# A SiLU-multiply kernel on one core: the body as one critical section with hand-written semaphores

## The chip, the cores and the metric

The kernel runs on one core of one Trainium2 chip. The metric is the device time in microseconds (us) of one execution. Before the change three executions took 471.06, 471.17 and 470.71 us; the median is 471.06.

The names of the engines in the profile: ACT is ScalarE, DVE is VectorE, POOL is GpSimd, SP is SyncE, and a q behind a name (SPq, ACTq) means the engine's sequencer, which issues DMAs and handles semaphores. This kernel does not use TensorE.

## The reference

The input has 32 x 512 rows of 2048 float32 numbers. Each row is split in two halves of 1024; the first goes through SiLU and is multiplied by the second. The output has the same rows with 1024 numbers each.

```python
x1, x2 = x[..., :half_dim], x[..., half_dim:]
silu_x1 = x1 * (1 / (1 + np.exp(-x1)))
return (silu_x1 * x2).astype(np.float32)
```

So 134.22 MB are read, 67.11 MB written, and each output element costs one activation and one multiply.

## The kernel before

The 16,384 rows are cut into 16 tiles of 1,024 rows. A tile holds K = 8 rows on each of the 128 partitions; two tiles (RUN = 2) share a group of rows, in which each partition owns 16 consecutive rows (`view`, line 42). There are two input buffers `xt` (64 KB for each partition) and two output buffers `ot` (32 KB for each partition); tile i uses buffer i % 2 of both.

For each tile:

- **load** (line 81): one DMA of 8 MB, issued by SP into `xt`, through the move helper, so that its line in the profile is L77.
- **compute** (line 91): ACT applies SiLU in place to the first half of each row in `xt` (L96); DVE multiplies it with the second half into `ot` (L102). A tile is one activation and one multiply of 128 x 8192 elements. Tile 0 is computed in four chunks of 2 rows (FIRST), the last tile in chunks of 2, 3 and 3 rows (LAST).
- **store** (line 109): one DMA of 4 MB, issued by ACT from `ot`, again L77. Tile 0 is stored by three DMAs over interleaved partitions (OPENING: every fourth from 0, every fourth from 2, every second from 1); the last tile by one DMA for each chunk.

Loads of tiles 0 and 1 come first. After that the load of tile i + 2 waits for tile i's multiply, which frees its input buffer, and the multiply of tile i waits for the store of tile i - 2, which frees its output buffer. Loads pass only through SP's DMA queue (q1 in the profile) and stores only through ACT's (q10).

The order of the work comes from three things. Within `manual_schedule` (line 45) ACT and DVE issue their instructions in the order in which the program writes them. All semaphores are set by the framework from the data that instructions share; it has one semaphore for each engine and a ring of eight for the DMAs, which the transfers take in turn. The kernel shapes these waits: `implied` (line 50) declares dependences that other waits already cover, so that no wait is made for them; `after` (line 58) fixes the order in which transfers take their semaphores (that order depends on `load_first`, line 125, which is true for tiles 4 to 7 and 12 to 15); and `settle_all_but` (line 66) gives SP an instruction that does nothing but wait for each earlier transfer and the last tile's multiplies ahead of the last transfer (its waits are on L67). At the end the framework waits on SP for what is still open and has all engines meet in a barrier, clear the semaphores and meet once more (these instructions are on L160, where its context closes). At the start all engines meet in a barrier as well (L149).

Of the kernel before, what the change touches and what calls it, by code (L numbers as in the profile page):

```python
# [1 line left out]

# [4 lines left out]


@with_exitstack
def kernel(  # L10
    ctx: ExitStack,
    tc: tile.TileContext,
    x: bass.AP,
    out: bass.AP,
):


    nc = tc.nc
    P = nc.NUM_PARTITIONS

    x_flat = x.flatten_outer_dims()
    out_flat = out.flatten_outer_dims()
    num_rows, in_cols = x_flat.shape
    half = in_cols // 2
    dt = x_flat.dtype

    K = 8
    FIRST = [2] * (K // 2)
    LAST = [2, 3, 3]
    OPENING = [  # L30
        (slice(0, None, 4), slice(None)),
        (slice(2, None, 4), slice(None)),
        (slice(1, None, 2), slice(None)),
    ]
    RUN = 2
    n_tiles = num_rows // (P * K)

    pool = ctx.enter_context(tc.tile_pool(name="pool", bufs=1))
    xts = [pool.tile([P, K, in_cols], dt, name=f"xt{b}") for b in range(2)]
    ots = [pool.tile([P, K, half], dt, name=f"ot{b}") for b in range(2)]  # L40

    def view(flat, i):
        return flat.rearrange("(g p t k) d -> g t p k d", p=P, t=RUN, k=K)[i // RUN, i % RUN]

    ctx.enter_context(tc.manual_schedule(engines={mybir.EngineType.Activation, mybir.EngineType.DVE}))

    sent = []
    loads, stores, silus, muls = {}, {}, {}, {}

    def implied(later, earlier, reason):  # L50
        for x in later:
            for y in earlier:
                tc.declare_no_dep(x, y, reason=reason)

    def earlier(done, i):
        return [ins for j in range(i % 2, i, 2) for ins in done[j]]

    def after(later, first):
        tc.add_manual_dep(
            later,  # L60
            first.name,
            mybir.DependencyInfo(mybir.DependencyClass.NoSync, mybir.DependencyReason.DATA),
            reason="order in which the transfers take their semaphores",
        )

    def settle_all_but(n, others):
        rest = nc.sync.nop(nofuse=True)  # L67
        for ins in sent[:-n] + others:
            tc.add_manual_dep(
                rest.ins,  # L70
                ins.name,
                mybir.DependencyInfo(mybir.DependencyClass.Sync, mybir.DependencyReason.DATA),
                reason="sync sees each earlier transfer land before the last ones",
            )

    def move(queue, out, in_):
        ins = queue.dma_start(out=out, in_=in_).ins  # L77
        sent.append(ins)
        return ins

    def load(i):
        loads[i] = [move(nc.sync, xts[i % 2][:], view(x_flat, i))]
        if i >= 2:
            implied(loads[i], earlier(loads, i), "the multiplies that this load awaits came after those loads")
            implied(loads[i], earlier(silus, i), "the multiplies that this load awaits came after those activations")

    def parts(sizes):
        assert sum(sizes) == K
        return [slice(sum(sizes[:n]), sum(sizes[:n + 1])) for n in range(len(sizes))]

    def compute(i, ot, chunks):
        xt = xts[i % 2]
        silus[i], muls[i] = [], []
        for ks in chunks:
            silus[i].append(
                nc.scalar.activation(  # L96
                    out=xt[:, ks, :half],
                    in_=xt[:, ks, :half],
                    func=mybir.ActivationFunctionType.Silu,
                ).ins  # L100
            )
            muls[i].append(nc.vector.tensor_mul(out=ot[:, ks], in0=xt[:, ks, :half], in1=xt[:, ks, half:]).ins)  # L102
        implied(muls[i], loads[i], "each multiply awaits an activation that came after the load")
        if i >= 2:
            implied(silus[i], earlier(silus, i), "the load that this activation awaits came after those activations")
            implied(silus[i], earlier(muls, i), "the load that this activation awaits came after those multiplies")
            implied(muls[i], earlier(muls, i), "the store that this multiply awaits came after those multiplies")

    def store(i, ot, pieces):
        ov = view(out_flat, i)  # L110
        stores[i] = [move(nc.scalar, ov[ps, ks], ot[ps, ks]) for ps, ks in pieces]

    ALL = slice(None)
    load(0)
    load(1)
    for i in range(n_tiles):
        ot = ots[i % 2]
        last = i == n_tiles - 1
        compute(i, ot, parts(FIRST if i == 0 else LAST if last else [K]))
        pieces = [(ALL, ALL)]  # L120
        if i == 0:
            pieces = OPENING
        elif last:
            pieces = [(ALL, ks) for ks in parts(LAST)]
        load_first = i // 4 % 2
        if load_first and i + 2 < n_tiles:
            load(i + 2)
        store(i, ot, pieces)
        if load_first and i + 2 < n_tiles:
            after(stores[i][0], loads[i + 2][0])  # L130
        if not load_first and i + 2 < n_tiles:
            load(i + 2)
            after(loads[i + 2][0], stores[i][-1])
    settle_all_but(1, muls[n_tiles - 1])


# [1 line left out]
_INS = ['x']  # L138
_OUTS = [((32, 512, 1024), 'float32')]


# [23 lines left out]
```

## Time and profile before

| what | us |
|---|---|
| median of the three times | 471.06 (470.71 to 471.17) |
| span of the profiled execution, first to last instruction | 469.19 |
| between the two: time around the span | 1.87 |
| ACT busy | 114.2 (24%) |
| DVE busy | 139.5 (30%) |
| share of the 16 DMA engines: loads, stores | 66.4%, 33.2% |
| activation of 128 x 8192 (L96), mean of 14 | 7.03 |
| multiply of 128 x 8192 (L102), mean of 14 | 8.69 |
| load of 8 MB, issue to landing, median | 42.2 |
| store of 4 MB, issue to landing, median | 42.0 |
| time of two tiles in the middle (one load issue to the next of the same buffer) | 58.0 |

The span runs from the program's first instruction to its last. The profiled execution is listed by its span alone; its own time lies above the span by about as much as the timed runs do, 1.87 us by their median. All times within the profile are counted from the start of the span.

How to read it: the page begins with the busy time of each engine, then gives the span in 40 equal slices with a digit for the busy share of each in tenths, and the DMA engines in the same way. A table of stretches gives the same for windows that one chooses. The chain of waits follows the work that ended last back to its start. The DMA issues list how long a transfer took from its issue until its semaphore said that it had landed. A DMA's time to landing includes the time that it stood in its queue behind others.

### The profile page before, as it was taken

What the parts mean: (1) busy time and instruction counts of PE and PEld (TensorE: products, weight loads), DVE (VectorE), ACT (ScalarE), POOL (GpSimd) and SP (SyncE); (2) the same over time, 40 slices, a digit from 0 to 9 for tenths busy, and PEclk for the clock granted to TensorE, in tenths of its full rate; (3) what the DMA queues carried; (4) which work ended last, traced back from release to release, by engine and by line L of the source; (5) the groups of instructions that cost most, each with busy time, mean ns of one, the idle gap of its engine ahead of it and who ended that gap; (6) DMA issues with size and microseconds to landing.
All of it is one profiled execution on the core that took longest, in us unless ns stands there. A gap on an engine that the chain in (4) does not pass through costs nothing.

```text
span 469.2 us, 156 instructions
## 1 busy us (share of the span) xinstructions
DVE 139.5 (30%) x21; ACT 114.2 (24%) x22; POOL 0.2 (0%) x4
## 2 busy tenths in 40 slices
DVE  0070522407034070330704307042070520605152
ACT  1051405032050410504105050050501405014060
POOL 0000000000000000000000000000000000000000
DMA  8999999999999999999999999999999999999998
GB/s 358 447 447 374 475 402 433 416 492 402 411 439 486 408 402 447 475 419 402 444 439 458 402 436 413 492 402 416 433 486 408 402 447 475 419 402 444 450 402 358
DMA packets 4928, 201.33 MB, mean 429 GB/s; under 512 B 576, under 2 KB 576, under 8 KB 576
## 3 DMA queue, kind: packets, MB, share of 16 engines
q1 hardware_dynamic: 2304, 134.22, 66.4%
q10 hardware_dynamic: 2624, 67.11, 33.2%
HBM read 134.22 MB, written 67.11 MB: 429 GB/s over the span
## 4 chain that ended last, share of the span: by engine, by line
DMA 72%; DVE 14%; ACT 11%; DVEq 1%; issue 0%; SPq 0%
DMA xt<-in_x_dram 72%; DVE ot L102 14%; ACT xt L96 11%; DVEq L160 1%; SPq L77 0%
## 5 line engine op out<-in xcount | busy, mean ns | idle before, releaser
L102 DVE TENSOR_TENSOR ot<-xt 128x8192 f32<-128x8192 f32 (+2 forms) x21 | 139.5, 6659 | 320.8 <-ACT xt L96 320.8
L96 ACT ACTIVATE xt<-xt 128x8192 f32<-128x8192 f32 (+2 forms) x21 | 112.9, 5400 | 341.4 <-DMA xt<-in_x_dram 341.4
L96 ACT ACT_TABLE_LOAD x1 | 1.3, 1283 | 0.7 <-PEq L149 0.7
L149 POOL MEMSET const-bfloat16-1.0<- 128x1 bf16 x1 | 0.1, 102 | 0.0
L149 POOL MEMSET const-uint8-127<- 128x1 uint8 x1 | 0.1, 102 | 0.0
L149 POOL MEMSET const-float32-0.0<- 128x1 f32 x1 | 0.1, 99 | 0.2 <-issue 0.2
L149 POOL MEMSET const-float32-1.0<- 128x1 f32 x1 | 0.1, 99 | 0.0
## 6 DMA issues: line engine op xcount, KB each, us to landing
out_dram<-ot ACTq DMA_DIRECT2D x14, 4096.0 KB, 42.0
out_dram<-ot ACTq DMA_DIRECT2D x3, 1024.0 KB, 12.0
out_dram<-ot ACTq DMA_DIRECT2D x2, 1536.0 KB, 7.9
out_dram<-ot ACTq DMA_DIRECT2D x1, 2048.0 KB, 37.2
xt<-in_x_dram SPq DMA_DIRECT2D x16, 42.2
```

The lines of the kernel that those rows point to most:

```text
L96: nc.scalar.activation(out=xt[:, ks, :half], in_=xt[:, ks, :half], func=mybir.ActivationFunctionType.Silu,).ins
L102: muls[i].append(nc.vector.tensor_mul(out=ot[:, ks], in0=xt[:, ks, :half], in1=xt[:, ks, half:]).ins)
L149: nc = _bacc.Bacc("TRN2", target_bir_lowering=False, num_devices=1)
L160: with _tile.TileContext(nc) as tc:
```

## The change

The framework's scheduling of the body is replaced by one critical section. The body is written once, in order, and every wait is written by hand. There are six semaphores: `acted` counts activations and `multiplied` multiplies; `loaded` and `stored` exist once for each buffer, and each transfer adds 16. What each engine waits for:

- ACT waits for a tile's load before its first activation, and for the multiplies before a store.
- DVE waits for the earlier stores from the same output buffer before a tile's first multiply, and for the activation before each multiply.
- SP waits for all multiplies of tile i before it issues the load of tile i + 2.
- GpSimd waits at the end until both `stored` counts are complete; it is the engine on which the section ends (`sync_engine`), and its own drain at that end is left out (`no_gpsimd_drain`).

The sizes of the tiles, the chunks, the pieces of the opening and last stores and the queues of the DMAs are the same. `manual_schedule`, the declared dependences, the order of semaphore slots with `load_first`, and `settle_all_but` go. In every tile the load is now written after the store.

```diff
-    ctx.enter_context(tc.manual_schedule(engines={mybir.EngineType.Activation, mybir.EngineType.DVE}))
...
-    settle_all_but(1, muls[n_tiles - 1])
+    with tc.tile_critical(sync_engine=mybir.EngineType.Pool, no_gpsimd_drain=True):
+        acted = ctx.enter_context(nc.semaphore("acted"))
+        multiplied = ctx.enter_context(nc.semaphore("multiplied"))
+        loaded = [ctx.enter_context(nc.semaphore(f"loaded{b}")) for b in range(2)]
+        stored = [ctx.enter_context(nc.semaphore(f"stored{b}")) for b in range(2)]
+        sent = [0, 0]
+        n_silu = n_mul = 0
+        def load(i):
+            nc.sync.dma_start(out=xts[i % 2][:], in_=view(x_flat, i)).then_inc(loaded[i % 2], 16)
+        load(0)
+        load(1)
+        for i in range(n_tiles):
...
+            nc.scalar.wait_ge(loaded[i % 2], 16 * (i // 2 + 1))
+            for ks in chunks:
                 nc.scalar.activation(
...
+                ).then_inc(acted, 1)
+            if i >= 2:
+                nc.vector.wait_ge(stored[i % 2], sent[i % 2])
+            done = []
+            for ks in chunks:
+                n_silu += 1
+                nc.vector.wait_ge(acted, n_silu)
+                nc.vector.tensor_mul(out=ot[:, ks], in0=xt[:, ks, :half], in1=xt[:, ks, half:]).then_inc(multiplied, 1)
+                n_mul += 1
+                done.append(n_mul)
+            pieces = [(ps, ks, n_mul) for ps, ks in OPENING] if i == 0 else [(ALL, ALL, n_mul)]
+            if last:
+                pieces = [(ALL, ks, n) for ks, n in zip(chunks, done)]
...
+            for ps, ks, n in pieces:
+                if n != awaited:
+                    nc.scalar.wait_ge(multiplied, n)
+                    awaited = n
+                nc.scalar.dma_start(out=ov[ps, ks], in_=ot[ps, ks]).then_inc(stored[i % 2], 16)
+                sent[i % 2] += 16
+            if i + 2 < n_tiles:
+                nc.sync.wait_ge(multiplied, n_mul)
+                load(i + 2)
+        for b in range(2):
+            nc.gpsimd.wait_ge(stored[b], sent[b])
```

More of the change, by code (lines that the diff above doesn't have):

```diff
@@ L43, in view @@
         return flat.rearrange("(g p t k) d -> g t p k d", p=P, t=RUN, k=K)[i // RUN, i % RUN]
-    ctx.enter_context(tc.manual_schedule(engines={mybir.EngineType.Activation, mybir.EngineType.DVE}))
[L47 to L85, printed above, removed]
     def parts(sizes):
@@ L89, in parts @@
         return [slice(sum(sizes[:n]), sum(sizes[:n + 1])) for n in range(len(sizes))]
[L91 to L95, printed above, removed]
+    ALL = slice(None)
+    with tc.tile_critical(sync_engine=mybir.EngineType.Pool, no_gpsimd_drain=True):
[5 more added lines that the diff above has]
+        n_silu = n_mul = 0
+        after_mul = []
+        def load(i):
[3 more added lines that the diff above has]
+        for i in range(n_tiles):
+            xt, ot = xts[i % 2], ots[i % 2]
+            last = i == n_tiles - 1
+            chunks = parts(FIRST if i == 0 else LAST if last else [K])
+            nc.scalar.wait_ge(loaded[i % 2], 16 * (i // 2 + 1))
+            for ks in chunks:
                 nc.scalar.activation(
@@ L99, in compute @@
                     func=mybir.ActivationFunctionType.Silu,
[L100 to L133, printed above, removed]
@@ new lines @@
+            if last:
+                pieces = [(ALL, ks, n) for ks, n in zip(chunks, done)]
+            ov = view(out_flat, i)
+            awaited = 0
+            for ps, ks, n in pieces:
[7 more added lines that the diff above has]
+                load(i + 2)
```

## The prediction

> **What bounds the kernel now.** I read the page first, then the table of stretches, the DMA issues, the chain of waits and at last the records at both ends. From the page, the busy rows and the chain:
>
> ```profile
> span 469.2 us, 156 instructions
> DVE 139.5 (30%) x21; ACT 114.2 (24%) x22; POOL 0.2 (0%) x4
> DMA  8999999999999999999999999999999999999998
> q1 hardware_dynamic: 2304, 134.22, 66.4%
> q10 hardware_dynamic: 2624, 67.11, 33.2%
> DMA 72%; DVE 14%; ACT 11%; DVEq 1%; issue 0%; SPq 0%
> ```
>
> The engines work 30% and 24% of the span; the 16 DMA engines work all of it: loads (q1) 66.4% and stores (q10) 33.2% make 99.6%. The chain gives DVE 14% and ACT 11%, but that is one buffer's chain: while tile 14 is multiplied, the other buffer's load keeps the DMA engines busy. The table of stretches (last two columns: DMA share, GB/s) shows it:
>
> ```profile
> 61.00:119.00 58.00, 17.52 (x3) 14.06 (x2) 0.00 (x0) 1.00 1.00 434
> 119.00:400.00 281.00, 80.08 (x10) 70.29 (x10) 0.00 (x0) 1.00 1.00 435
> 448.00:460.00 12.00, 8.62 (x3) 7.22 (x3) 0.00 (x0) 1.00 1.00 431
> ```
>
> The DMA share is 1.00 at 434 to 435 GB/s even from 448 to 460, where the last tile is computed. So the time is three pieces: until the first packet, 201.33 MB of packets, and what follows the last landing. The packet records put the first packet at 1.73 us and the end of the last at 468.04, 466.3 us of the span's 469.19. At 434 GB/s throughout, the bytes would take 463.9; the other 2.4 lie at the start (slices of 325 and 379 GB/s from 2 to 6 us), at the opening stores (346 and 335 GB/s from 36 to 40) and in the uneven finish after 466.
>
> How much cover there is, from the timeline and the chain's end:
>
> ```profile
> 406.86 0.33 SPq L77 DMA_DIRECT2D xt<-in_x_dram  x1
> 453.35 0.34 ACTq L77 DMA_DIRECT2D out_dram<-ot  x1
> 457.07 3.60 ACTq L77 DMA_DIRECT2D out_dram<-ot  x2
> 406.86 42.19 DMA xt<-in_x_dram
> 457.04 3.27 DVEq L160
> ```
>
> The load of tile 15 is issued at 406.86; by the semaphore records the load ahead of it lands at 419.94. It could be issued 13.1 us later before the load queue ran out. At the end tile 14's store lands at 458.63 and tile 15's three pieces at 461.08, 464.74 and 468.38, each right behind the one before. The first packet follows an issue by 1.0 us (issue 0.73, packet 1.73), so the pieces, issued at 453.35, 457.07 and 460.33, could each come about 4.3, 3.0 and 3.4 us later without a gap.
>
> **What the change removes.** The waits of the sync queue, in us:
>
> ```profile
> SPq L77 <- DVE ot L102: 400.0, 14, 31.9
> SPq L67 <- DMA out_dram<-ot: 44.5, 1, 44.5
> SPq L67 <- DMA xt<-in_x_dram: 12.9, 1, 12.9
> SPq L160 <- DMA out_dram<-ot: 3.5, 1, 3.5
> ```
>
> SP's nop with its waits (L67) is done at 464.86, 3.5 us before the last landing, so its removal saves nothing; what is late next is the last landing, as now. SP's 12 and ACT's 3 separate semaphore instructions on L77 take 17 ns each, with 10 us and more to spare: nothing. The declared dependences and the order of semaphore slots are no instructions. In tiles 4 to 7 and 12 to 15 the load was written ahead of the store and now stands behind it, but loads go through SP's queue and stores through ACT's, both wait for the same multiply (406.86 and 406.87 above), and no transfer passes another in its queue.
>
> **What it adds inside.** Per tile a wait on ACT for the load and one for the multiply, on DVE one for the stores two tiles back and one for the activation, on SP one for the multiply; five more of the kind stand at the chunks of tiles 0 and 15. Today most of these conditions ride on the instruction itself, so each is either folded in again (nothing) or a separate instruction. The nearest rows are steps between neighbouring sequencer instructions at L160: SP 0.055 to 0.062 us, GpSimd 0.078, ACT 0.092, DVE 0.110. From landing to next load issue three of them follow one another: at most 0.055 + 0.092 + 0.110 = 0.26 us a tile, against 13.1 us of cover. Behind ACT's wait for the multiply are the store and the next activation, as now; behind DVE's wait for stores the multiply, and the stores have landed by then (the ones that tile 2 needs at 71.94, its activation starts at 72.15). So I count 0; if the cover were gone it would be 16 x 0.26 = 4.1 us. At the end two such steps a piece (0.2 us) stand against 3.0 us. The table load of ACT (1.28 us, now at 0.72) may come to stand behind the first wait for data. Then tile 0 ends 1.3 us later, and load 2 is issued at 34.8 instead of 33.5, while load 1 lands at 45.36: 10.5 us of cover are left, again 0.
>
> **What it adds at the start.** Nothing is outstanding when the section is entered, so each engine enters by itself. Between the opening barrier and load 0 I count one more SP step, 0.06 us. Bounds: nothing, and a whole barrier round, which in the rows of the end takes 0.46 us (GpSimd's release at 468.62 to its next at 469.08). I take the step, since nothing earlier is there to wait for.
>
> **What it adds at the end.** Now, from the instruction records: the last landing releases SP at 468.40, its two drains follow at 468.46 and 468.51, GpSimd sees them at 468.55, and two barrier rounds end at 469.19. The rows of that line:
>
> ```profile
> L160 POOLq EVENT_SEMAPHORE  x4: 17/17/17, 468.5 to 469.1; - x4
> L160 SPq EVENT_SEMAPHORE  x3: 17/17/17, 468.4 to 469.1; - x3
> L160 SPq DRAIN  x3: 7/7/7, 468.5 to 468.8; - x3
> L160 POOLq EVENT_SEMAPHORE_RANGE_CLEAR  x1: 93/93/93, 468.8 to 468.8; - x1
> ```
>
> In the changed kernel GpSimd is released instead. After its wait I count a branch out, a placeholder in its drain's stead and the section's end: 3 x 0.078 = 0.23 us. The other engines' drains at the section's end wait for compute that ended by 460.3, so they cost nothing. Then SP has to learn of it (GpSimd's release at 468.62 reached SP's wait at 468.665, 0.04) and goes on as today: +0.27, say 0.28. Bounds: if GpSimd joins the barrier straight from its wait, SP's three steps fall away, -0.15; if the end also needs a barrier round of its own, 0.28 + 0.46 = +0.74. I take 0.28, whose rows are those of this very place.
>
> [...]
>
> **Sum.** 469.19 + 0.06 + 0.28 = 469.53 of span. The median of the timed runs is 471.06, 1.87 above the span (the single times, 470.71 to 471.17, 1.5 to 2.0); I leave these 1.87 as they are: 469.53 + 1.87 = **471.4 us**.
>
> **The rivals.**
> 1. *The new steps take the place of the old* (folded waits, GpSimd straight into the barrier, or an edit that leaves the order of events as it is): +0 - 0.15, 470.9 to 471.1. For it: the same engine leads the barrier. Against it: a section's end is work that has to sit somewhere.
> 2. *Barrier rounds at entry and exit*: 0.46 + 0.74 = +1.2, 472.3. Against it: nothing is outstanding at the entry, and the exit is told to skip GpSimd's drain.
> 3. *Slower, by code that has to be fetched.* If the section's code is not on the engine when SP enters it or GpSimd leaves it, the fetch stands fully on the path: load 0 isn't out yet, and the last landing is past. Nearest rows: all 13 packets of the instruction queue lie before the span, those of 8 KB take 0.32 to 0.53 us, and a transfer's first packet came 1.0 us after its issue; one fetch is 1.4 us, an estimate from these. One gives 471.4 + 1.4 = 472.8, both 474.2. It decides from a single miss on, since 1.4 is over the 0.94 us that are 0.2%. For it: GpSimd would leave the section after hundreds of us of waiting. Against it: every stream is short (156 records for all engines), and no instruction packet falls inside the span of before.
> 4. *Faster*: the opening stores meet the loads otherwise and the dip at 36 to 40 us (0.86 us) goes, perhaps with the start's 0.75. 469.8 to 470.5. Against it: same three pieces, same queues, same trigger.
>
> [...]
>
> **How the numbers follow.** Forecast 0.72, rival 1 0.12, rival 2 0.06, rival 3 0.06, rival 4 0.04. A measurement of this kernel can tell about 0.2%, 0.94 us, from no change: 470.12 to 472.00. Forecast and rival 1 lie inside, and rival 4 with its first dip alone. Rival 4 gives half of its 0.04 to each side, rivals 2 and 3 lie above: faster 0.02, same 0.72 + 0.12 + 0.02 = 0.86, slower 0.12. The range goes from rival 1's low end less the scatter of a run (470.9 - 0.35, about 470.5) to rival 2 (472.3, about 472.4); rival 3 and most of rival 4 are left out.
>
> **What would show it.** Right: the DMA share stays 1.00 at 434 GB/s from 61 to 460 us, the first packet comes at 1.7 to 1.9, the last landing about 466.6 us after it, and 0.9 to 1.2 us follow instead of 0.81. A wait inside that cost something would show as a stretch below 0.99. Rival 2 would show as a pair of extra semaphore steps on all engines before load 0; rival 3 as instruction-queue packets inside the span and a gap of over 1 us after the last landing or before load 0; rival 4 as 434 GB/s from 36 to 40. A DMA share below 1.00 between 458 and 466 would prove the cover at the end wrong, and with it the whole sum.

## The result and the profile after

The changed kernel takes **471.63 us** (median of 20 executions, 471.33 to 471.90) against 471.00 for the kernel before (20 executions, 470.68 to 471.36): 0.63 us more, a ratio of 1.0014 (95% interval 1.0008 to 1.0021). The forecast was 471.4 with a range of 470.5 to 472.4. Executions more than 1.5% above the fastest of their kernel are left out of every comparison.

The page of the changed kernel, the same lines as before:

```profile
span 469.9 us, 151 instructions
DVE 139.5 (30%) x21; ACT 114.2 (24%) x22; POOL 0.2 (0%) x4
DMA  8999999999999999999999999999999999999988
q1 hardware_dynamic: 2304, 134.22, 66.2%
q10 hardware_dynamic: 2624, 67.11, 33.1%
```

The work of every engine and the bytes are the same, and the table of stretches (last two columns: DMA share, GB/s) shows the same full middle:

```profile
61.00:119.00 58.00, 17.52 (x3) 14.06 (x2) 0.00 (x0) 1.00 1.00 434
119.00:400.00 281.00, 79.88 (x10) 70.29 (x10) 0.00 (x0) 1.00 1.00 435
448.00:460.00 12.00, 8.45 (x3) 7.22 (x3) 0.00 (x0) 1.00 0.98 423
```

The last of these reads 0.98 and 423 where it read 1.00 and 431 before. By the packet records, with each packet's bytes spread over its own duration, the stretch is full in both kernels, at 432 GB/s. So the difference lies at the ends. Cut into three pieces by the records of the two profiled executions:

| piece, us | before | after | difference |
|---|---|---|---|
| start of the span to the issue of load 0 | 0.731 | 0.880 | +0.149 |
| issue of load 0 to the last landing | 467.653 | 467.645 | -0.008 |
| last landing to the end of the span | 0.803 | 1.362 | +0.559 |
| span | 469.187 | 469.887 | +0.700 |

That the middle agrees to 0.008 us is partly chance: over the nine other profiles with a full middle it lies between 467.46 and 467.96. The ends don't scatter like that. The six other profiles that leave the changed kernel's start alone have 0.87 to 0.88 us ahead of load 0, the five that leave its end alone 1.35 to 1.36 behind the last landing; the three other profiles of the kernel before have 0.73 ahead of load 0.

The time around the span is the same: 1.78 us in the mean over the 20 executions after, 1.79 over 27 of before.

**The start.** The chain of waits of the kernel before, then of the changed one (start, us, what):

```profile
0.67 0.07 issue
0.73 0.37 SPq L77
```

```profile
0.61 0.02 POOLq L114
0.62 0.06 issue
0.69 0.02 POOLq L50
0.71 0.02 issue
0.73 0.03 SPq L125
0.76 0.12 issue
0.88 0.37 SPq L60
```

Two steps are new: a marker on GpSimd (0.69, L50) and a branch on SP that waits for it (0.73, L125). By the instruction records SP leaves the opening barrier at 0.65 in both kernels. Its next instruction follows 0.08 us later in both; before, that was load 0, and now it is the branch. So the marker costs nothing that shows, and the 0.15 us from the branch to load 0 are the whole loss.

**The end.** The records of the section's line, L50 (GpSimd's sequencer is POOLq; count, durations in ns, first and last start):

```profile
L50 POOLq NOP  x3: 13/13/13, 0.7 to 469.1; - x3
L50 POOLq EVENT_SEMAPHORE  x3: 17/17/43, 468.8 to 469.0; - x3
L50 POOLq COMPARE_BRANCH  x1: 33/33/33, 468.6 to 468.6; - x1
L50 SPq DRAIN  x1: 7/7/7, 468.8 to 468.8; - x1
L50 ACTq DRAIN  x1: 8/8/8, 468.8 to 468.8; - x1
L50 DVEq DRAIN  x1: 10/10/10, 468.8 to 468.8; - x1
```

All of it but the first placeholder (NOP, at 0.7: the marker of the entry) stands behind the last landing, the drains of SP, ACT and DVE too, although those engines had nothing left to do. One after the other on GpSimd: released at 468.549; branch at 468.615; a signal to the other engines at 468.760; a placeholder for its drain at 468.856; two waits for the three drains at 468.949 and 469.015; the section's end at 469.106. Then SP's two drains, at 469.145 and 469.205, and the barrier on GpSimd at 469.270. That is 0.72 us from release to barrier, where the kernel before took 0.14.

**The middle.** Of the waits written by hand for the tiles only one kind is an instruction of its own, on DVE ahead of the multiplies of tiles 2 to 15 (L80, 14 times, 21 ns each); the rest rode on other instructions. The kernel before had more of them: 15 on DVE (L102), 12 on SP and 3 on ACT. But DVE's stood ahead of the activation's end and now follow it: in tile 14 the multiply starts 0.11 us after the activation (427.26 to 427.37) where it took 0.03 (427.17 to 427.20). That is the whole delay inside, and the load queue covers it. SP's and ACT's issues follow the multiply as closely as before:

```profile
398.35 8.69 DVE L81 TENSOR_TENSOR ot<-xt 128x8192 f32<-128x8192 f32 x1 [20.33 <-ACT xt L70]
407.07 0.33 SPq L60 DMA_DIRECT2D xt<-in_x_dram  x1
407.07 0.36 ACTq L93 DMA_DIRECT2D out_dram<-ot  x1
```

### The profile page after: what moved, and what is told of

Same layout as the page of the kernel before. It is cut to its first block, busy times and chain, and to the rows that moved or that the text cites. A ratio compares the mean times of both kernels' runs of the same rounds, so it can differ in the third digit from the quotient of the medians.

```text
span 469.9 us, 151 instructions
## 1 busy us (share of the span) xinstructions
DVE 139.5 (30%) x21; ACT 114.2 (24%) x22; POOL 0.2 (0%) x4
## 3 DMA queue, kind: packets, MB, share of 16 engines
q10 hardware_dynamic: 2624, 67.11, 33.1%
## 4 chain that ended last, share of the span: by engine, by line
DMA 72%; DVE 14%; ACT 11%; issue 0%; SPq 0%; DVEq 0%; POOLq 0%
DMA xt<-in_x_dram 72%; DVE ot L81 14%; ACT xt L70 11%; SPq L60 0%; DVEq L80 0%; SPq L125 0%; POOLq L50 0%; POOLq L114 0%
```

## The experiments

The theory after the result: the whole loss is sequencer steps that stand in a row ahead of load 0 and behind the last landing. Rivals: GpSimd is the wrong engine for the end; a boundary costs wherever it stands; delays in the middle are paid for in part.

**Another engine at the end** (`sp_end`).

```diff
-    with tc.tile_critical(sync_engine=mybir.EngineType.Pool, no_gpsimd_drain=True):
+    with tc.tile_critical(sync_engine=mybir.EngineType.SP, no_gpsimd_drain=True):
...
-            nc.gpsimd.wait_ge(stored[b], sent[b])
+            nc.sync.wait_ge(stored[b], sent[b])
```

> The changed kernel with SP instead of GpSimd as the engine that awaits the last stores and on which the section ends. Theory (the whole loss is sequencer steps in a row at the two ends; the round at the section's end costs about the same on any engine): SP's steps are 0.055 to 0.062 us where GpSimd's are 0.066 to 0.11, and the hop from GpSimd to SP goes, so the 1.34 us after the last landing become 1.1 to 1.2; span 469.6 to 469.8, time 0.4 to 0.6 us above before. Rival (it is GpSimd that is slow): back to before's 0.79 us after the last landing, span 469.2 to 469.3.

Measured: 471.55 us, ratio to before 1.0014 (1.0005 to 1.0023). After the last landing 1.23 us instead of 1.36, load 0 issued at 0.94 instead of 0.88; span 469.75. The steps are nearly the same, with one wait fewer, and now on SP's sequencer:

```profile
L50 SPq NOP  x2: 13/13/13, 0.7 to 469.0; - x2
L50 SPq EVENT_SEMAPHORE  x2: 17/22/28, 468.8 to 468.9; - x2
L50 SPq COMPARE_BRANCH  x1: 33/33/33, 468.6 to 468.6; - x1
```

The end fell by 0.13, and the start gave 0.06 of it back, since SP now sets the marker itself ahead of its branch. GpSimd is not what costs most; the expected 1.1 to 1.2 behind the landing was a little low, and so were the expected 0.4 to 0.6 above before (0.66 between the medians).

**One more section ahead of it** (`empty_first`).

```diff
+    with tc.tile_critical(sync_engine=mybir.EngineType.Pool, no_gpsimd_drain=True):
+        for engine in (nc.sync, nc.scalar, nc.vector, nc.gpsimd):
+            engine.nop(nofuse=True)
     with tc.tile_critical(sync_engine=mybir.EngineType.Pool, no_gpsimd_drain=True):
```

> The changed kernel with one more critical section ahead of it, which holds one empty instruction on each of SP, ACT, DVE and GpSimd. Theory (an entry and an exit cost what their steps take in a row where nothing hides them): the exit's steps from the branch on took 0.49 us, the entry's 0.15, so load 0 is issued 0.6 us later, at 1.5 instead of 0.88, and the span is 470.5. Rival (the loss belongs to the final wait, a bare section is free): 469.9 to 470.0.

Measured: 472.71 us (5 executions), 1.08 more than the changed kernel. The chain now reaches load 0 at 1.60, 0.72 later, after a second branch:

```profile
1.39 0.02 SPq L128
1.41 0.04 issue
1.45 0.03 SPq L128
1.48 0.12 issue
1.60 0.37 SPq L63
```

The mean span of its executions is 470.62, against 469.85 for the changed kernel: 0.77 more. A bare boundary where nothing hides it costs some 0.7 to 0.8. The rest, 0.25 us in the mean, lies around the span (2.03 instead of 1.78), which neither theory had.

**The same boundary in the middle** (`two_halves`).

```diff
-        for i in range(n_tiles):
+        for i in range(n_tiles // 2):
...
+    with tc.tile_critical(sync_engine=mybir.EngineType.Pool, no_gpsimd_drain=True):
+        for i in range(n_tiles // 2, n_tiles):
```

> The changed kernel with the section closed after tile 7 and opened again for tiles 8 to 15, without a wait for transfers between. Theory: exit and entry cost the same 0.6 us there, but the load queue holds 13 us of cover, so the span stays at 469.9, within 0.1, and the DMA share stays 1.00 through the middle. Rival (a boundary costs wherever it stands): 470.5.

Measured: 471.76 us. The mean span is 469.75, not longer than the changed kernel's 469.85, and the stretch around the boundary (at 233.6, when tile 7 is multiplied) is full:

```profile
224.00:252.00 28.00, 8.69 (x1) 5.99 (x2) 0.00 (x0) 1.00 0.99 431
```

The same steps that cost 0.7 ahead of load 0 cost nothing here that the runs can tell. The 0.13 us by which the time is longer lies around the span (2.02), as in `empty_first`.

**GpSimd's drain** (`pool_drain`).

```diff
-    with tc.tile_critical(sync_engine=mybir.EngineType.Pool, no_gpsimd_drain=True):
+    with tc.tile_critical(sync_engine=mybir.EngineType.Pool):
```

> The changed kernel with GpSimd's own drain at the section's end, which the change leaves out. Theory: one more drain on GpSimd between the last landing and the end; drains of GpSimd in the trace take 0.03 to 0.18 us, so span 469.9 to 470.1. Rival (a drain of GpSimd is dear, and leaving it out is what keeps the loss this small): 471 or more.

Measured: 471.63 us, and 1.383 us after the last landing instead of 1.362. Leaving the drain out is worth 0.02 us, a little under the expected 0.03 to 0.18: the drain takes 0.041 us where the placeholder takes 0.013.

**The round of the engines, or the steps of one** (`wait_own`).

```diff
+    with tc.tile_critical(sync_engine=mybir.EngineType.SP, no_gpsimd_drain=True):
         for b in range(2):
-            nc.gpsimd.wait_ge(stored[b], sent[b])
+            nc.sync.wait_ge(stored[b], sent[b])
```

> The changed kernel with the section closed right after its last store's issue, and the two waits for stores in a second section of their own on SP alone. Theory (the round of the four engines at a section's end costs only because it stands behind the last landing): it now runs at 460.5 us, 8 us ahead of the last landing, and is hidden; behind the landing stay SP's wait, its branch out (0.15) and one or two steps of 0.06, so 1.0 to 1.1 us instead of 1.36, span 469.5 to 469.7. The time outside the span may be 0.24 longer, as in the two kernels with two sections. Rival (the branch and the end's bookkeeping cost it on any engine, not the round): 1.25 us or more, span 469.8 or more.

Measured: 471.53 us, and 1.253 us after the last landing. The four engines' round was over at 461.4. But the second section's end, on SP alone, has a branch, a signal, a drain and a placeholder of its own (L98), and waits on the framework's line:

```profile
L98 SPq NOP  x2: 13/13/13, 461.5 to 469.3; - x2
L98 SPq EVENT_SEMAPHORE  x1: 17/17/17, 469.1 to 469.1; - x1
L98 SPq DRAIN  x1: 7/7/7, 469.2 to 469.2; - x1
```

Here the rival was right, if barely (1.25 or more, it said). Its twelve spans, with a median of 469.75, lie between the two expectations. The fair comparison is `sp_end`, where SP also waits last but with the round of all engines behind the landing: 1.228 there, 1.253 here. Hiding the round saved nothing; the 0.11 us against the changed kernel are those of SP in GpSimd's place (0.13 in `sp_end`). So the loss fits the number of steps on the engine that was released last, whether or not it talks to others.

**The cover in the middle** (`half_more`, `one_more`, `two_more`): DVE multiplies a part or the whole of tiles 1 to 14 again, each time waiting for itself. The output is the same. `half_more` was planned after the other two had run. For `one_more` (`two_more` does it twice, `half_more` on rows 0 to 3 alone):

```diff
             for ks in chunks:
                 n_silu += 1
                 nc.vector.wait_ge(acted, n_silu)
+                for _ in range(1 if 0 < i < n_tiles - 1 else 0):
+                    nc.vector.tensor_mul(out=ot[:, ks], in0=xt[:, ks, :half], in1=xt[:, ks, half:]).then_inc(multiplied, 1)
+                    n_mul += 1
+                    nc.vector.wait_ge(multiplied, n_mul)
```

> The changed kernel in which DVE multiplies the first four rows of tiles 1 to 14 once more (the result is the same), so that about 4.5 us are added between each landing and the next load's issue. Theory (what is added inside is hidden while the load queue has some 5 us left for the spread of the 16 DMA engines; 13.1 - 4.5 leaves 8.6): span 469.7 to 470.1, and no load's first and last engine land more than 1 us apart. Rival (any delay inside is paid for in part, as with the whole multiply): 472 or more.

> The changed kernel in which DVE does the multiply of tiles 1 to 14 twice (the result is the same; DVE waits for the first of them), so that 8.7 to 8.8 us are added between each landing and the next load's issue. Theory (the load queue holds 13.1 us of cover): span 469.7 to 470.1, the DMA share in the middle stays 1.00. Rival (what is added inside costs time): up to 14 x 8.7 = 122 us more; a tenth of that would already show as 12 us.

> The same with the multiply of tiles 1 to 14 done three times: 17.5 us added for each tile. Theory: that is 4.4 us more than the cover of 13.1, so the load queue runs dry each time; stores fill a part of it, so the loss lies between a few us and 14 x 4.4 = 62 us; span 475 to 532, DMA share in the middle 0.88 to 0.99. If the cover is larger than it looks: 470 again.

`half_more`: 471.56 us, the time of the changed kernel; each load's first and last engine land at most 0.43 us apart. 14 x 4.4 us of delay cost nothing:

```profile
61.00:119.00 58.00, 28.45 (x5) 14.06 (x2) 0.00 (x0) 1.00 1.00 434
119.00:400.00 281.00, 122.21 (x20) 70.29 (x10) 0.00 (x0) 1.00 1.00 435
```

`one_more` did not bear out the expectation. Its four executions took 472.63, 492.03, 492.24 and 496.26. Even the shortest has a span of 470.9, above the expected 469.7 to 470.1 and 1.0 above the changed kernel's. The profile is of one of the three long ones, 492.03:

```profile
61.00:119.00 58.00, 35.72 (x6) 14.06 (x2) 0.00 (x0) 1.00 1.00 426
119.00:400.00 281.00, 164.08 (x19) 63.26 (x9) 0.00 (x0) 1.00 1.00 414
```

The DMA share is still 1.00, but at 414 GB/s. A share of 1.00 is no proof of full rate: 392 of the 2048 packets of 64 KB took over 1.1 times the usual 2.418 us, against 29 in the changed kernel. Summed up, the packets of all kinds took 17.2 us more for each of the 16 engines, most of the 20.4 us by which the span is longer. And the engines fall out of step: a load's first and last engine land up to 4.1 us apart (0.45 in the changed kernel). Yet no engine had run dry: from load 4 on, when a load is issued, the first engine is still 1.4 to 4.5 us and the last 5.0 to 7.0 us from landing the load ahead, and load 0's first packet came 1.0 us after its issue (0.88 to 1.88 in the changed kernel). No other kernel here has an execution more than 0.6% above its fastest, so the short cover probably has a part in it; that it causes the slow packets is not shown, and why they come, and not in every execution, stays open.

`two_more`: 543.14 us (2 executions), the span 541.6, the DMA share from 60 us on 0.81 to 0.91. The loss, 72 us, is over the expected 62 at most (475 to 532), and the waits show another cause than the one I had written:

```profile
ACT xt L70 <- DVE ot L85: 240.1, 9, 26.7
ACT xt L70 <- DMA xt<-in_x_dram: 170.8, 7, 27.4
```

ACT's store waits for the multiply and stands ahead of the next activation, so a tile is one activation and three multiplies in a row, 7.0 + 26.1 = 33.1 us, more than the 29.0 of the DMA engines: most loads come every 33.7 us, and most are issued after the load ahead has landed.

**The end of the kernel before, by steps** (`no_settle`, `settle_silu`). Both are the kernel before with one line changed; the first leaves out `settle_all_but`, the second adds to it.

```diff
-    settle_all_but(1, muls[n_tiles - 1])
+    settle_all_but(1, muls[n_tiles - 1] + silus[n_tiles - 1])
```

> The kernel before without the instruction by which SP sees the earlier transfers land ahead of the last one. Theory (the end is the number of sequencer steps that stand behind the last landing): SP's waits for those transfers, some four or five of 0.06 us, now stand in the framework's end; if the last landing is awaited first, 0.2 to 0.3 us more than 0.80 follow it, span 469.4; if it is awaited last, 469.2 as before. Rival (the waits for what has landed long ago are free): 469.2.

> The kernel before in which that instruction also awaits the last tile's activations, so that the framework's end needs no wait for ACT. Theory (steps): one drain of SP, 0.055 us, goes from between the last landing and the end: 0.75 instead of 0.80 us; too little for the timed runs to show. Rival: 0.80 as before.

Measured: without it 471.15 us (ratio 1.0008, 0.9999 to 1.0017) and 0.991 us after the last landing, 0.188 more than before; with more in it 470.98 (1.0002, 0.9993 to 1.0011) and 0.753, 0.050 less. SP's waits, first without it, then with more in it:

```profile
SPq L159 <- DMA out_dram<-ot: 61.2, 1, 61.2
```

```profile
SPq L67 <- DMA out_dram<-ot: 44.6, 1, 44.6
SPq L160 <- DMA out_dram<-ot: 3.5, 1, 3.5
```

Without it, SP stands for 61.2 us at the framework's line until the last landing, and three further semaphore instructions for what had landed long before follow it, 0.06 us each. A wait that is already met is not free when it stands behind the last landing. The timed runs can't tell either kernel from before; the traces can.

**The opening** (`one_opening`): the kernel before with `OPENING = [(slice(None), slice(None))]`.

> The kernel before with tile 0 stored by one DMA instead of three over interleaved partitions. If the dip to 346 and 335 GB/s at 36 to 40 us belongs to the three pieces, it goes and the span is 0.8 shorter (468.4). If it belongs to the first meeting of stores and loads, whatever their pieces: 469.2 again. If the pieces were of use in spreading that meeting: a deeper dip and 469.5 or more.

Measured: 471.02 us, ratio 1.0005 (0.9996 to 1.0014). By the packet records the dip is still there, 353 and 350 GB/s at 36 to 40 us. So it is not the pieces' doing. That it belongs to the first meeting of stores and loads fits, but only these two ways of storing tile 0 were run.

## Why the prediction was right, and where it was not

- **The bound** was right: load 0's issue to last landing is 467.65 us in both profiles, so the time is a start, a stretch of transfers that the change leaves alone, and an end.
- **What is removed saves nothing**: right. SP's settling ended 3.5 us ahead of the last landing. But it had shortened the end: without it three waits follow the landing (+0.19, `no_settle`).
- **The added waits cost 0**: right. They delay a tile's multiply by less than 0.1 us, and 4.4 us a tile would also have cost nothing (`half_more`). What did not hold is the size of the cover, "it could be issued 13.1 us later": with 8.7 us used up the executions lost 1 to 25 us, before the load queue had run dry in the one that was profiled (`one_more`). The sum did not hang on it. The reading had a slip too: the landing at 419.94 is that of a store, and load 14 lands at 420.11. The table load of ACT stayed ahead of its first wait, at 0.89.
- **The start, +0.06 forecast, +0.15 measured**: the term was "one more SP step", read from neighbouring rows since the trace of before has no branch, and a branch is not one step of 0.06 us. "Each engine enters by itself" was wrong as well, since SP's branch waits for GpSimd's marker, but that cost nothing here. The trace has the branches on SP, ACT and GpSimd as rows of 33 ns, but 153 ns pass from the start of SP's to load 0, 146 from ACT's to its table load and 145 from GpSimd's at the end to its signal: the idle time after a branch counts with it.
- **The end, +0.28 forecast, +0.56 measured**: the failed step is "three times 0.078" = 0.23 from GpSimd's release to the section's end. There it took 0.56, because six steps stood there and not three, and the branch took 0.145. The claim that the other engines' drains cost nothing holds for the drains themselves, which are over by 468.82, 0.13 us before GpSimd comes to wait for them. What it missed is that GpSimd starts them by a signal after its own wait and then passes two waits for them: three more steps. The hop to SP was right (0.04), and from the section's end to the barrier 0.16 passed, about as forecast.
- **The rivals**: that nothing is added (1) and that code must be fetched (3) are refuted: the steps are in the trace, and all 13 packets of the instruction queue begin before the span, as in the kernel before. Rival 2 (entry 0.46, end 0.74, 472.3) had the kind of cost right, with a branch on each engine that waits for the marker and a round of the engines at the end, and its size too high: 0.15 and 0.56. Rival 4's dip did not go (352 and 318 GB/s at 36 to 40 us), and is not the pieces' doing.
- **The signs**: by the packet records the DMA engines stayed full to 466, the first packet came at 1.88 and the last landing 466.64 after it, all as named. The one for the end failed: 1.36 us follow the last landing and not 0.9 to 1.2.
- **Sum**: +0.34 forecast, +0.70 in the span, +0.63 between the medians. Both terms were too small, since I counted only the steps that I could name, and the best value was half of what came. The 1.87 around the span, taken from two different executions, was 0.09 too large, which hid a little of the miss. The class was right because both ends were bounded by rows of the same place, and 0.63 lies under the 0.94 us that the prediction counted as no change. The interval leaves out 1, so the small loss is real.

No version here beats the kernel before by more than the runs can tell. Waits for the last stores in the framework's own part, behind the section, were not tried.

## What to carry to other kernels

Where the DMA engines are full throughout, as here (467.65 us from load 0's issue to the last landing in both profiles), only what stands ahead of the first issue and behind the last landing counts: count the sequencer instructions there (in these traces each 0.06 us on SP and 0.07 to 0.1 on GpSimd, a branch 0.15), and move what can be moved to before the last landing, waits that are already met included (three of them took 0.19 us in `no_settle`). A section boundary cost 0.7 to 0.8 us in the open and nothing that shows in the middle. When you state how much delay a queue hides, leave room: 4.4 us of 13 were free here, 8.7 were not.

## What the runs showed of the hardware that was not expected

- Of the first 16 packets of load 0, 12 take 3.1 to 3.3 us in the changed kernel instead of the usual 2.4, and 16 packets at 36 to 37 us take 3.2 to 3.5. In `two_more`, where the load queue is empty or nearly so each time, 15 or 16 packets of 3.2 to 4.6 us follow each load's issue from 78.7 us on.
- Two kernels with a second section over the four engines have 0.24 us more around the span (2.02 and 2.03 instead of 1.78); `wait_own`, whose second section holds SP alone, has not (1.79). The cause is open.
